# RWKV-7 and sparse-attention block on one core: half-array matmuls issued one half after the other instead of in turns

## The chip, the core and the metric

The kernel runs on one core of a Trainium2 chip. A core has a matrix engine (TensorE, PE in the profile, whose weight loads are listed apart as PEld), a vector engine (VectorE, DVE), an activation engine (ScalarE, ACT), a general engine (GpSimd, POOL) and a queue engine that issues DMAs (SyncE, SP). The metric is the device time of one launch in microseconds, the median of several runs; one execution is profiled as well.

## What is computed

One transformer block for 512 tokens of width 2048: a linear-recurrence mixer (RWKV-7, 16 heads of 64), an attention with three branches (compressed, selected, window; 16 query heads in 4 groups, head width 64), a gated mix of both, an MLP of width 8192, and RMS norms. What the change touches, cut to its core:

```
# the recurrence, per head and token; the kernel does it in chunks of 64 tokens
S = S * w_t + sa (kk_t * a_t)^T + v_t k_t^T        # sa = -S kk_t
y = S r_t

# attention, per head; q 512x64, keys and values 512x64
s = q k^T * scale - slope * dist                   # causal, masked
p = softmax(s)
o = p v                                            # gated sum of the branches
```

In chunk form the recurrence needs, for each head and chunk, the products of the scaled keys with the scaled queries (keys by queries), a triangular inverse, and two products that the text calls Z (scores times values) and W (inverse times keys).

## The kernel before

All data stands with features on the 128 partitions. Two heads of width 64 share one set of partitions: head 0 on partitions 0 to 63, head 1 on 64 to 127. Many of the products are therefore matmuls on half of the 128x128 array. There are three kinds of halves here: 64 rows of the array (a contraction over 64, written 64\*128 in the profile), 64 columns (an output of 64 partitions, 128\*64), or both (64\*64).

**Stages.** Stage 1 (`stage1`, 35 to 985 us of the span) goes over 8 pairs of heads: `gates` prepares a pair, `inner` does the work of the chunks that needs no state, `outer` runs over the 8 chunks in order. Stage 2 does the compressed keys and then `attention` (1150 to 1442 us). Stage 3 does the output projections and the MLP, 1674 us long, and the change doesn't touch it.

**Order.** PE and POOL run in the order in which the code is written. Between the pieces of `inner`, `outer` and `attention`, `pump` puts pieces of the large projections (three matmuls of 128x512 a time, L104 to L106) by a credit that the code counts, so PE has projection work to do while DVE and ACT work on the heads. DVE, ACT and SP in stage 1 and 2 are ordered by a scheduler.

**The four groups.**

- L634, in `inner_a`: keys by queries. For each half b of the 8 chunks, four chunks and two heads: the head picks the rows of the array (`hs`), and each head has an output tile of its own (`pS[h]`, named `un` in the trace). 8 pairs x 2 halves = 16 groups of 8 matmuls, 128 columns streamed each.
- L724, in `inner_b`: Z. Four pairs of chunks `cp` and the two chunks `q` of each; `q` picks rows and columns, so these are quarter arrays, 64 columns streamed. 16 groups of 8 matmuls (8 pairs, 2 heads).
- L733, in `inner_b` for the second head: W. Four `cp` and two heads; the head picks the output columns (`hs`), 128 columns streamed. 8 groups of 8 matmuls.
- L1043, in `att_c`: P V. For query tile i (0 to 3) of 128 queries, the key tiles b from 0 to i and two heads; the head picks the output columns, 128 columns streamed, and the products for all b are added up in one place. 8 pairs of heads x 2 branches x 4 tiles = 64 groups of 2(i+1) matmuls, 320 in all.

Every one of them is a matmul of f32 data, and each such matmul leaves two records in the trace (640 for the 320 of L1043), one behind the other.

Of the kernel before, what the change touches and what calls it, by code (L numbers as in the profile page):

```python
# [52 lines left out]
class Kern:  # L53
# [568 lines left out]
    def inner_a(self, cur):  # L622

        nc, p, pp = self.nc, self.p1, self.ps1
        AR, KB, S = cur["AR"], cur["KB"], cur["S"]
        sts = []
        for b in range(2):
            self.pump(PUMP["s"])
            pS = [pp.tile([128, 4, 128], F32, name="un", bufs=3) for h in range(2)]
            for i in range(4):  # L630
                c = 4 * b + i
                for h in range(2):
                    hs = slice(64 * h, 64 * h + 64)
                    nc.tensor.matmul(pS[h][:, i], KB[hs, c // 2, c % 2].rearrange("p a t -> p (a t)"),  # L634
                                     AR[hs, :, C * c:C * c + C], start=True, stop=True)
            for h in range(2):
                nc.vector.tensor_tensor(S[:, h, 4 * b:4 * b + 4].rearrange("p (a b) t -> p a b t", b=2),
                                        pS[h].rearrange("p (a b) t -> p a b t", b=2),
                                        self.mk[:, 0:2].unsqueeze(1).to_broadcast([128, 2, 2, 128]), OP.mult)
        for h in range(2):  # L640

            st = dict(h=h, NT=S[:, h, :, 0:64].rearrange("p (a b) t -> p a b t", b=2))
            X = self.masked(st, 2, F16, "X", nc.vector)
            st["DT"] = p.tile([128, 4, 128], F16, name=f"D{h}1")
            nc.vector.tensor_tensor(st["DT"], self.identb, X, OP.subtract)
            st["X"] = X
            sts.append(st)
        return sts
# [65 lines left out]
    def inner_b(self, h, cur, st):  # L714

        nc, p, pp = self.nc, self.p1, self.ps1
        S, VU, An, WT, DT = cur["S"], cur["VU"], cur["An"], cur["WT"], st["DTf"]
        hs = slice(64 * h, 64 * h + 64)
        pZ = pp.tile([128, 4, C], F32, name="un", bufs=3)
        for cp in range(4):  # L720
            for q in range(2):
                ds, ks = slice(64 * q, 64 * q + 64), slice(64 - 64 * q, 128 - 64 * q)
                c = 2 * cp + q
                nc.tensor.matmul(pZ[ds, cp], S[ks, h, c, 0:64], VU[ks, c, hs], start=True, stop=True)  # L724
        st["Z"] = p.tile([128, 4, C], F32, name="Z", bufs=1)
        nc.scalar.copy(st["Z"], pZ)
        if h == 0:
            cur["DT0"] = DT
            return
        pW = pp.tile([128, 4, 128], F32, name="un", bufs=3)  # L730
        for cp in range(4):
            for hs, dt in ((slice(0, 64), cur["DT0"]), (slice(64, 128), DT)):
                nc.tensor.matmul(pW[hs, cp], An[:, cp, hs], dt[:, cp], start=True, stop=True)  # L733
        nc.scalar.copy(WT, pW)

# [301 lines left out]
    def att_c(self, j, i, br):  # L1037
        nc = self.nc
        pT = self.pT.pop((j, i, br))
        for b in range(i + 1):  # L1040
            for h in range(2):
                v0 = 256 * br + 64 * (2 * (j // 4) + h)
                nc.tensor.matmul(self.o[j][64 * h:64 * h + 64, 128 * i:128 * i + 128], self.vn[:, b, v0:v0 + 64],  # L1043
                                 pT[h][:, b], start=False, stop=i == 3 and br == 1 and b == 3)
        if i == 3 and br == 1:
            t = self.p2.tile([128, T], F32, name="z", bufs=2)
            nc.scalar.copy(t, self.o[j])
            nc.sync.dma_start(self.yd[8 + j], t)
# [501 lines left out]
```

## Time and profile before

| | |
|---|---|
| Median of 3 runs | 3124.81 us (3119.63 to 3130.18) |
| Profiled execution, own time | 3125.73 us |
| its span, first to last instruction | 3124.0 us |
| PE busy | 3050.8 us, 98% |
| DVE, ACT, POOL busy | 1855.4, 1192.9, 588.6 us |
| DMA | 369.28 MB, mean 118 GB/s |

PE is busy nearly all the time in every one of the 40 slices. "Busy" is the union of the records of an engine: two matmul records that overlap are counted once, so a group whose mean record is long and whose busy time is short ran several at a time. "Idle before" is the time in which the engine stood still just ahead of a group, with what ended it.

### The profile page before, as it was taken

The numbers are of one execution on the slowest core, as the hardware profiler recorded it, in microseconds if no ns is written. First come the engines' busy times: TensorE is split into PE (matmuls) and PEld (weight loads), VectorE is DVE, ScalarE is ACT, GpSimd is POOL, SyncE is SP. The second block draws the span as 40 slices with busy tenths as digits, with TensorE's granted clock in tenths as the row PEclk, the third lists the DMA queues.
The fourth block names the chain that finished last, engine by engine and source line by source line (L and its number), as shares of the span: only waits on it lengthen the run. The fifth ranks groups of instructions, "written<-read, shape, count | busy, mean of one in ns | idle before, by whom it ended". The sixth has DMA issues, their size and how long they took to land.

```text
span 3124.0 us, 49657 instructions
## 1 busy us (share of the span) xinstructions
PE 3050.8 (98%) x19296; PEld 2591.8 (83%) x19296; DVE 1855.4 (59%) x3312; ACT 1192.9 (38%) x2031; POOL 588.6 (19%) x613
## 2 busy tenths in 40 slices
PE   9999999999999999999999899999999999999998
PEld 7777777777777877787888899999997888888998
DVE  7855756575563457775464877777775232344565
ACT  4322333233232335654333444444444232232454
POOL 2312222231231000001221533333330000000012
PEclk9999999999999999999999999999999999999999
DMA  4222222222224422225543344444446243253465
GB/s 163 82 85 75 82 78 74 71 82 83 77 79 142 135 95 65 65 78 189 169 144 128 133 135 128 131 135 134 128 130 204 94 139 103 94 165 118 148 193 176
DMA packets 165596, 369.28 MB, mean 118 GB/s; under 512 B 18672, under 2 KB 24304, under 8 KB 157168
## 3 DMA queue, kind: packets, MB, share of 16 engines
q1 hardware_dynamic: 154080, 339.28, 33.7%
q10 hardware_dynamic: 10640, 24.73, 2.1%
q8 instruction: 151, 2.47, 0.3%
q0 software_dynamic: 640, 2.10, 0.2%
q14 instruction: 85, 0.70, 0.1%
HBM read 322.06 MB, written 41.94 MB: 117 GB/s over the span
## 4 chain that ended last, share of the span: by engine, by line
PE 62%; DVE 2%; DMA 1%; POOL 1%; issue 0%; ACT 0%; SPq 0%; DVEq 0%; ACTq 0%; POOLq 0%
PE acc L1263 20%; PE acc L104 13%; PE acc L106 12%; PE acc L105 12%; PE po L1043 1%; PE sc L1010 1%; PE pt L1032 1%; DMA wraw<-w_down 1%; DVE wlo L68 0%; DMA u<-ud 0%; PE sc L954 0%; POOL rb L1177 0%; DMA raw<-w_up 0%; PE po L989 0%; POOL sq L1175 0%
## 5 line engine op out<-in xcount | busy, mean ns | idle before, releaser
L67 ACT CAST whi<-wraw 128x512 fp32r<-128x512 f32 x752 | 465.8, 620 | 1065.9 <-PE acc L105 989.2
L68 DVE TENSOR_TENSOR wlo<-wraw,whi 128x512 fp32r<-128x512 f32 x752 | 530.7, 707 | 567.6 <-ACT whi L67 560.0
L104 PE MATMUL acc<-xn,whi 128*128 128x512 f32 x1472 | 611.5, 415 | 1.3 <-DVE th L387 1.3
L106 PE MATMUL acc<-xn,wlo 128*128 128x512 f32 x1472 | 578.2, 393 | 0.0
L105 PE MATMUL acc<-xn,whi 128*128 128x512 f32 x1472 | 577.1, 392 | 0.0
L104 PE MATMUL acc<-xs,whi 128*128 128x512 f32 (+1 forms) x1280 | 449.5, 351 | 5.4 <-ACT xs L932 5.4
L105 PE MATMUL acc<-xs,whi 128*128 128x512 f32 (+1 forms) x1280 | 449.1, 351 | 2.0 <-DVE xs L933 2.0
L106 PE MATMUL acc<-xs,wlo 128*128 128x512 f32 (+1 forms) x1280 | 448.8, 351 | 0.1
L1263 PE MATMUL acc<-hx,hs 128*128 128x256 f32 x2048 | 369.8, 283 | 3.1 <-ACT hs L1248 3.1
L106 PEld LDWEIGHTS acc<-xn,wlo 128*128 128x128 f32 x1472 | 277.3, 188 | 61.6
L104 PEld LDWEIGHTS acc<-xn,whi 128*128 128x128 f32 x1472 | 278.1, 189 | 60.0 <-issue 6.5
L1263 PEld LDWEIGHTS acc<-hx,hs 128*128 128x128 f32 x2048 | 317.4, 190 | 3.3 <-ACT hs L1248 3.3
L105 PEld LDWEIGHTS acc<-xn,whi 128*128 128x128 f32 x1472 | 278.7, 189 | 46.0
L1263 PE MATMUL acc<-hx,ls 128*128 128x256 f32 x1024 | 289.2, 282 | 2.1 <-DVE ls L1249 2.1
L1263 PE MATMUL acc<-hx,h 128*128 128x256 f32 x1536 | 277.8, 283 | 5.0 <-ACT h L1240 5.0
L104 PEld LDWEIGHTS acc<-xs,whi 128*128 128x128 f32 x1280 | 241.4, 189 | 41.2 <-ACT xs L932 6.4
L105 PEld LDWEIGHTS acc<-xs,whi 128*128 128x128 f32 x1280 | 241.4, 189 | 38.4 <-DVE xs L933 3.5
L106 PEld LDWEIGHTS acc<-xs,wlo 128*128 128x128 f32 x1280 | 241.4, 189 | 35.5 <-DVE wlo L68 0.5
L1263 PEld LDWEIGHTS acc<-hx,h 128*128 128x128 f32 x1536 | 237.7, 190 | 5.4 <-ACT h L1240 5.4
L1249 DVE TENSOR_TENSOR ls<-s,hs 128x1024 fp32r<-128x1024 f32 x128 | 184.5, 1441 | 74.6 <-ACT hs L1248 74.5
L1263 PE MATMUL acc<-hx,l 128*128 128x256 f32 x768 | 216.5, 282 | 1.8 <-DVE l L1241 1.8
L1263 PEld LDWEIGHTS acc<-hx,ls 128*128 128x128 f32 x1024 | 195.8, 191 | 2.3 <-DVE ls L1249 2.3
(354 smaller groups left out, 4225.3 us busy)
## 6 DMA issues: line engine op xcount, KB each, us to landing
wraw<-w_down SPq DMA_DIRECT2D x320, 256.0 KB, 3.2
raw<-w_up SPq DMA_DIRECT2D x64, 1024.0 KB, 5.2
wraw<-w_gate SPq DMA_DIRECT2D x128, 256.0 KB, 3.0
wraw<-w_rkv SPq DMA_DIRECT2D x96, 256.0 KB, 3.1
wraw<-w_o SPq DMA_DIRECT2D x64, 256.0 KB, 3.1
ud<-f ACTq DMA_DIRECT2D x32, 512.0 KB, 6.2
u<-ud SPq DMA_DIRECT2D x32, 512.0 KB, 5.3
thd<-th SPq DMA_DIRECT2D x32, 256.0 KB, 3.5
```

What stands on the lines that cost most here:

```text
L67: nc.scalar.copy(hi, raw)
L68: lo_eng.tensor_tensor(lo, raw, hi.bitcast(F32), OP.subtract)
L104: nc.tensor.matmul(ps, hi[:, j], xh, start=opens and k == 0, stop=False)
L105: nc.tensor.matmul(ps, hi[:, j], xl, start=False, stop=False)
L106: nc.tensor.matmul(ps, lo[:, j], xh, start=False, stop=close and last)
L1010: nc.tensor.matmul(ps[:, 0:n], q, self.kst[h][:, x, br, 0:n], start=x == 0, stop=x == 1)
L1032: nc.tensor.transpose(pt[:, b], s[:, 128 * b:128 * b + 128], self.ident)
L1043: nc.tensor.matmul(self.o[j][64 * h:64 * h + 64, 128 * i:128 * i + 128], self.vn[:, b, v0:v0 + 64], pT[h][:, b], start=False, stop=i == 3 ...
L1249: nc.vector.tensor_tensor(l, s, h.bitcast(F32), OP.subtract)
L1263: nc.tensor.matmul(o, w[wi][part][:, 128 * i:128 * i + 128], x[:, xi, xp], start=kh == 0 and i == 0 and m == 0 and slot in opens, stop=kh ...
```

## The change

In all four groups the two loops are exchanged: the loop that picks the half of the array is now the outer one. The same matmuls run on the same data into the same places; no instruction is added or taken away.

```diff
         for b in range(2):                                  # inner_a
             pS = [pp.tile([128, 4, 128], F32, name="un", bufs=3) for h in range(2)]
-            for i in range(4):
-                c = 4 * b + i
-                for h in range(2):
+            for h in range(2):
+                for i in range(4):
+                    c = 4 * b + i
                     hs = slice(64 * h, 64 * h + 64)
                     nc.tensor.matmul(pS[h][:, i], KB[hs, c // 2, c % 2].rearrange("p a t -> p (a t)"),
                                      AR[hs, :, C * c:C * c + C], start=True, stop=True)
...
-        for cp in range(4):                                 # inner_b
-            for q in range(2):
+        for q in range(2):
+            for cp in range(4):
                 ds, ks = slice(64 * q, 64 * q + 64), slice(64 - 64 * q, 128 - 64 * q)
                 c = 2 * cp + q
                 nc.tensor.matmul(pZ[ds, cp], S[ks, h, c, 0:64], VU[ks, c, hs], start=True, stop=True)
...
-        for cp in range(4):
-            for hs, dt in ((slice(0, 64), cur["DT0"]), (slice(64, 128), DT)):
+        for hs, dt in ((slice(0, 64), cur["DT0"]), (slice(64, 128), DT)):
+            for cp in range(4):
                 nc.tensor.matmul(pW[hs, cp], An[:, cp, hs], dt[:, cp], start=True, stop=True)
...
-        for b in range(i + 1):                              # att_c
-            for h in range(2):
+        for h in range(2):
+            for b in range(i + 1):
                 v0 = 256 * br + 64 * (2 * (j // 4) + h)
                 nc.tensor.matmul(self.o[j][64 * h:64 * h + 64, 128 * i:128 * i + 128], self.vn[:, b, v0:v0 + 64],
                                  pT[h][:, b], start=False, stop=i == 3 and br == 1 and b == 3)
```

On PE, P V of query tile 3 (i = 3) of the first pair of heads, before. `po` is the output, `pT_11725` and `pT_11732` the softmax probabilities of head 0 and head 1, `vn` the values:

```order
L1032 MATMUL pt_11787<-ident_58,s_11600 128x128 x4
L1032 MATMUL pt_11794<-ident_58,s_11606 128x128 x4
L1043 MATMUL po_11243<-pT_11725,vn_9871 64x128
L1043 MATMUL po_11243<-pT_11732,vn_9871 64x128
L1043 MATMUL po_11243<-pT_11725,vn_9871 64x128
L1043 MATMUL po_11243<-pT_11732,vn_9871 64x128
L1043 MATMUL po_11243<-pT_11725,vn_9871 64x128
L1043 MATMUL po_11243<-pT_11732,vn_9871 64x128
L1043 MATMUL po_11243<-pT_11725,vn_9871 64x128
L1043 MATMUL po_11243<-pT_11732,vn_9871 64x128
L104 MATMUL acc_11740<-hn3_9861,whi_11588 128x512
```

The same place after:

```order
L1032 MATMUL pt_11787<-ident_58,s_11600 128x128 x4
L1032 MATMUL pt_11794<-ident_58,s_11606 128x128 x4
L1043 MATMUL po_11243<-pT_11725,vn_9871 64x128 x4
L1043 MATMUL po_11243<-pT_11732,vn_9871 64x128 x4
L104 MATMUL acc_11740<-hn3_9861,whi_11588 128x512
```

The four matmuls of head 0 now stand in a row, then the four of head 1; what is ahead and behind is unchanged. L634 and L733 move in the same way (`un_1272` and `un_1273` there are the outputs of the two heads), and L724 too, whose rows read alike for both halves. On DVE the scheduler answers with a small move in `inner_a` of each pair: the evacuations of keys by queries (L637, `S`), and what is made of them for the inverse (L652 `X`, L645 `D`; 0 and 1 are the heads), beside a piece of the projections' weights (L68):

```order
 L637 TENSOR_TENSOR S_1263<-un_1296,masks_753 128x512
+L652 TENSOR_TENSOR X0_1308<-S_1263,masks_753 128x512
 L637 TENSOR_TENSOR S_1263<-un_1297,masks_753 128x512
-L652 TENSOR_TENSOR X0_1308<-S_1263,masks_753 128x512
+L645 TENSOR_TENSOR D01_1310<-ident_58,X0_1308 128x512
 L652 TENSOR_TENSOR X1_1312<-S_1263,masks_753 128x512
-L645 TENSOR_TENSOR D01_1310<-ident_58,X0_1308 128x512
+L68 TENSOR_TENSOR wlo_1324<-wraw_1322,whi_1323 128x512
 L645 TENSOR_TENSOR D11_1314<-ident_58,X1_1312 128x512
-L68 TENSOR_TENSOR wlo_1324<-wraw_1322,whi_1323 128x512
```

Head 0's steps come ahead of head 1's evacuation, and one weight split moves ahead of the last step of head 1. ACT, POOL and SP keep their order.

## Rows read from the trace of the kernel before

**Rows 1.** The page: busy time by engine; granted clock over 40 slices.

```profile
PE 3050.8 (98%) x19296; PEld 2591.8 (83%) x19296; DVE 1855.4 (59%) x3312; ACT 1192.9 (38%) x2031; POOL 588.6 (19%) x613
...
PEclk9999999999999999999999999999999999999999
```

**Rows 2.** Busy time in stage 1 and in the attention; columns as named.

```profile
core 0: us, PE busy (x) PEld busy (x) DVE busy (x) ACT busy (x) POOL busy (x), PEclk, DMA share, GB/s
35.00:985.00 950.00, 926.87 (x6017) 715.99 (x6016) 586.82 (x1160) 293.78 (x548) 241.83 (x338) 1.00 0.25 82
...
1130.00:1450.00 320.00, 313.88 (x2058) 252.76 (x2058) 220.93 (x769) 175.95 (x487) 15.54 (x19) 1.00 0.26 83
```

**Rows 3.** What PE waited for: us in total, times, longest; attention, then stage 1.

```profile
PE sc L954 <- DVE sm L1012: 3.5, 7, 0.6
...
PE big L619 <- ACT sq L612: 13.8, 10, 3.9
PE un L677 <- DVE D L689: 3.3, 12, 0.3
PE un L677 <- DVE D L663: 1.3, 1, 1.3
```

**Rows 4.** Groups by line: shapes, count, busy us, mean ns, idle before.

```profile
L1043 PE MATMUL po<-pT,vn 128*64 128x128 f32 x640 | 49.1, 283 | 0.0
L1032 PE MATMUL pt<-ident,s 128*128 128x128 f32 x320 | 45.6, 273 | 0.0
```

**Rows 5.** Timeline of PE, P V: start us, us, engine, line, records; three places.

```profile
1300.09 1.09 PE L1043 MATMUL po<-pT,vn 128*64 128x128 f32 x16
1301.11 0.50 PE L104 MATMUL acc<-hn,whi 128*128 128x512 f32 x1
...
1305.90 0.44 PE L1043 MATMUL po<-pT,vn 128*64 128x128 f32 x4
1306.27 0.50 PE L104 MATMUL acc<-xn,whi 128*128 128x512 f32 x1
...
1313.01 0.66 PE L1043 MATMUL po<-pT,vn 128*64 128x128 f32 x8
1313.60 0.50 PE L104 MATMUL acc<-xn,whi 128*128 128x512 f32 x1
```

**Rows 6.** Timeline of PE in `outer`, and of the compressed keys (L888).

```profile
162.75 0.29 PE L572 MATMUL py<-S,VU 128*64 128x64 f32 x4
...
164.55 0.43 PE L550 MATMUL seq<-M,WT 128*64 128x128 f32 x2
...
1006.46 0.42 PE L888 MATMUL po<-h,cw 128*64 128x31 f32 x4 [0.34 <-ACT kbd L890]
```

**Rows 7.** Timeline of PE in `inner`: L702, then Z (L724) and W (L733).

```profile
149.33 1.11 PE L702 MATMUL un<-Df,N 128*128 128x128 f32 x8
150.19 0.48 PE L104 MATMUL acc<-xn,whi 128*128 128x512 f32 x1
...
154.99 0.68 PE L724 MATMUL un<-VU,S 64*64 64x64 f32 x16
155.60 1.09 PE L733 MATMUL un<-Q,An 128*64 128x128 f32 x16
156.63 0.51 PE L104 MATMUL acc<-xn,whi 128*128 128x512 f32 x1
```

**Rows 8.** Timeline of PE, keys by queries (L634), and of DVE there.

```profile
114.87 1.16 PE L634 MATMUL un<-AR,KB 64*128 64x128 f32 x16
115.96 0.50 PE L104 MATMUL acc<-xn,whi 128*128 128x512 f32 x1
...
121.15 1.28 DVE L645 TENSOR_TENSOR D<-ident,X 128x512 f16<-128x512 f32 x2
122.36 0.68 DVE L68 TENSOR_TENSOR wlo<-wraw,whi 128x512 fp32r<-128x512 f32 x1
```

**Rows 9.** What ended DVE's waits at L637, whole span: us, times, longest.

```profile
DVE S L637 <- PE un L634: 11.5, 10, 1.4
```

**Rows 10.** Stretches around a drop of the granted clock; columns as in rows 2.

```profile
437.60:439.40 1.80, 0.57 (x5) 0.57 (x6) 0.07 (x1) 1.24 (x3) 0.40 (x2) 0.97 0.37 133
439.40:443.00 3.60, 3.60 (x11) 2.81 (x11) 3.60 (x7) 0.42 (x1) 0.00 (x0) 0.54 0.26 84
```

## Prediction

> **What bounds the kernel now.** I read the busy times first. PE is busy 3050.8 of 3124.0 us, the next engine 59% [rows 1], and the two stages that the change touches look the same: PE 926.87 of 950 us in stage 1, 313.88 of 320 us in the attention [rows 2]. Then PE's waits: in the attention the largest is 3.5 us in all, in stage 1 it is 13.8 us at L619, behind a chain of small operations at the end of each pair of heads, and a few us at L677 [rows 3]. So PE's own time sets the end here, its order is written by hand, and a microsecond that a group on PE takes longer is a microsecond of the end, unless it stands in a place where PE would have waited anyway.
>
> **How fast the groups run now.** Line sums show something odd: P V (L1043) has 640 records of mean 283 ns in only 49.1 us, the transposes (L1032), with as many columns streamed, have 320 records of mean 273 ns in 45.6 us [rows 4]. Twice the records in about the same time: two halves of the array work at once. The timeline gives the price. A group of 16 records starts at 1300.09 and the next matmul at 1301.11, 1.02 us; a group of 4 takes 1305.90 to 1306.27, 0.37 us [rows 5]. Twelve records more cost 0.65 us. I call one turn, in which each half takes one record, a step: six more steps, 0.108 us each, and 0.37 - 2 x 0.108 = 0.15 us that a group pays once. A whole-array f32 matmul with the same columns, L702, takes 149.33 to 150.19 for 8 records, 0.1075 us each [rows 7]. So a step of two halves costs what one record costs on the whole array; the second half rides for free.
>
> The other groups read likewise. W (L733): 155.60 to 156.63, 1.03 us for 16 records, the same 0.108 a step. Z (L724): 154.99 to 155.60, 0.61 us; less 0.15, by 8 steps, 0.058 us (at most 0.61/8 = 0.076) [rows 7]. Keys by queries (L634): 114.87 to 115.96, 1.09 us [rows 8]; less 0.15 that is 0.1175 a step, and L702's 0.1075 is the floor; I take 0.112.
>
> **What the change does to that.** It removes and adds nothing. Within a half the records were one behind the other before, too, so the price of a step for one half is known from the same rows. What changes is who stands next to whom. With n matmuls per half, before there were 2n steps (two records each, both halves together). After, half A's 2n records stand ahead of half B's. If nothing of them overlaps, there are 4n steps; if all of it does, still 2n. The question is how far PE lets a matmul of the other half pass matmuls that wait for their own half.
>
> Three rows bear on it. Two records of one half alone, L550, take 0.43 us from first start to last end, and four records of two halves, the 4-record group of L1043, take 0.44 us [rows 5, 6]. In the second case the program's order is A, B, and each is two records. Were B's first record held until A's second had begun, the group would have three steps, 0.108 us more. It has two: B passes at least one waiting record of A, so two neighbouring matmuls of different halves overlap whole. And four records of one half, L888, take 0.42 us with 31 columns, where four records of two halves, L572, take 0.29 us with 64 columns [rows 6]: within one half nothing overlaps.
>
> In the new order A and B are neighbours once in each group: A's last matmul and B's first. By what the rows show, those two overlap, and the other n - 1 of each half run alone. A group then has 2n + 2(n - 1) steps, 2(n - 1) more than before. That is my forecast:
>
> - L634, n = 4: 16 groups x 6 steps x 0.112 = 10.8 us.
> - L724, n = 4: 16 x 6 x 0.058 = 5.6 us (7.3 at 0.076).
> - L733, n = 4: 8 x 6 x 0.108 = 5.2 us.
> - L1043, n = i + 1: for each of 16 (pair, branch) 0 + 2 + 4 + 6 = 12 steps, 16 x 12 x 0.108 = 20.7 us. At i = 0 the order doesn't change.
>
> Sum 42.3 us, half in stage 1 and half in the attention.
>
> What could take some of it back: PE's waits in these stages. L619 comes after a chain that begins behind `inner`, so its 13.8 us stay. The 3.5 us at L954, where PE waits for DVE to empty a score tile, can shrink, since DVE gains slack; L677 with 4.6 us likewise [rows 3]. At most 8 us, likeliest near nothing, since the extra work stands behind these waits' causes and not between cause and wait. DVE gets head 0's scores earlier than head 1's and its waits at L637 (11.5 us in 10 times [rows 9]) move, but it is busy only 586.82 of the 950 us of stage 1 [rows 2]. In DVE's new order a weight split, 0.68 us, stands ahead of the last `D` of head 1 [rows 8]; that `D` is first used behind `pump` with some five pieces of projection of 0.7 us, which hide it. Without that cover it would be 8 x 0.68 = 5.4 us. I take zero for each, and -8 to +5 us into the range.
>
> The profiled execution took 3125.73 us, 0.9 us over the median; 3125.7 + 42.3 - 0.9 = 3167 us.
>
> **Rivals.**
>
> *Hardly any overlap at the border.* A's last records may be under way before B's first is looked at. Then L634 pays 8 steps a group (14.3 us), L724 7.4, L733 6.9, and L1043 4 + 6 + 8 = 18 steps for i = 1 to 3, 31.1 us: 60 us, 3185. With one record overlapping, about 51 us. For it: nothing in the trace shows the border itself. Against it: the 4-record group. The Trainium skill, "TensorE: Matmul & The Clock Gate", Part 3 (The mechanism), states that matmuls start and end strictly in program order and only weight loads are pulled ahead; by that rule this rival would hold, but the 4-record group, 0.44 us against 0.43 us of two records, disagrees with it.
>
> *The two halves still run together; not slower.* If PE looks far ahead, B's first record starts beside A's first, although seven records of A (n = 4) stand between them. Every group keeps its 2n steps and the change does nothing: 0 us, 3125, with -4 for DVE's earlier start. It decides at the depth of that look: with 7 waiting records passed all groups are whole, with 3 passed the groups of n = 2 are whole, and n = 4 pays 4 steps instead of 6, n = 3 two: 7.2 + 3.7 + 3.5 + 16 x 6 x 0.108 = 24.8 us, 3150. For it: B demonstrably passes one record. Against it: no row shows more than one, because before A and B never stand further apart. The same page's table of TensorE's queue gives it a depth of 64 and a partial reorder window; taken at its word for matmuls, it would give this rival's 3125, and no run here shows it.
>
> *The clock falls.* In 439.40 to 443.00 the granted clock was 0.54, the lower of the two levels (1.2 instead of 2.4 GHz), behind a stretch in which PE was busy 0.57 of 1.80 us [rows 10]; that cost about 3.6 x 0.46 = 1.7 us. If PE at work with half of its array let the clock fall too, each of the 32 long groups of the attention could bring it, 54 us beside the 42: 3221. Against it: PE stays busy in all of them, L1043 runs beside whole-array work, and the page's clock is near full everywhere [rows 1].
>
> *Faster by more than the noise.* Head 0's scores are done half a group earlier. The gain is bounded by PE's waits at L677, 4.6 us, so it can't be seen.
>
> **How the numbers follow.** Forecast (border of one matmul, 3159 to 3174): 0.42. Hardly any overlap (3175 to 3188): 0.20. Deeper look, part of the cost (3138 to 3158): 0.12. Full overlap (3121 to 3130): 0.21. Clock: 0.03. Anything faster by over 0.3%: 0.02. About 0.3%, 9.4 us, is what a measurement of this kernel can tell from no change. So slower 0.42 + 0.20 + 0.12 + 0.03 = 0.77, same 0.21, faster 0.02. Without the full overlap the range would leave out 0.26, so it reaches there: 3121 to 3188; given that the kernel gets slower at all, I expect 3148 to 3188.
>
> **What would show it.** The mean record of the four lines stays (283 ns for P V); the busy time of L1043 goes from 49.1 to about 70 us (49 by the full overlap, 80 without any). A 16-record group of L1043 goes from 1.02 to 1.67 us (1.02 by full overlap, 1.88 with none at the border), L634 from 1.09 to 1.76, L733 from 1.03 to 1.68, L724 from 0.61 to 0.96, and the 4-record group stays at 0.37. The 8-record group (n = 2, 0.59 us from 1313.01 to 1313.60 [rows 5]) decides the depth: 0.81 us by the forecast, unchanged if B passes three records. Stage 3 and the waits of PE stay within a few us. I am wrong if the groups lengthen and the end doesn't move as much, for then PE's time was not the bound, or if a wait of another engine on these groups grows beside them.

## The result: 0.93% slower, seven tenths of the forecast

The changed kernel takes 3153.65 us in the median of 4 runs (3151.15 to 3157.55), against 3123.82 us of the kernel before (3119.63 to 3130.18): 1.0093 times as long, 95% interval 1.008 to 1.0106, or 29.8 us more. The forecast was 3167 us with a range of 3121 to 3188. The direction was right, and so was what bounds the kernel, PE's own time; the size was 13 us too large, because PE overlaps the two halves further than the forecast had it.

The page of the changed kernel, its busy times and the granted clock, beside [rows 1]:

```profile
span 3149.4 us, 49651 instructions
...
PE 3078.2 (98%) x19296; PEld 2619.6 (83%) x19296; DVE 1856.8 (59%) x3312; ACT 1193.5 (38%) x2031; POOL 589.1 (19%) x613
...
PEclk9999999999999999999999999999999999999999
```

The same number of matmul records keeps PE busy 27.4 us longer, and the span is 25.4 us longer. The other engines do what they did. The four groups, first as they were before (shapes, count, busy us, mean ns of one, idle before; L1043 stands in [rows 4]):

```profile
L634 PE MATMUL un<-AR,KB 64*128 64x128 f32 x256 | 18.7, 285 | 0.0
L724 PE MATMUL un<-VU,S 64*64 64x64 f32 x256 | 10.9, 224 | 0.0
L733 PE MATMUL un<-Q,An 128*64 128x128 f32 x128 | 8.8, 279 | 0.0
```

and in the changed kernel:

```profile
L1043 PE MATMUL po<-pT,vn 128*64 128x128 f32 x640 | 61.3, 283 | 0.0
...
L634 PE MATMUL un<-AR,KB 64*128 64x128 f32 x256 | 27.4, 285 | 0.0
L724 PE MATMUL un<-VU,S 64*64 64x64 f32 x256 | 15.4, 224 | 0.0
L733 PE MATMUL un<-Q,An 128*64 128x128 f32 x128 | 12.6, 279 | 0.0
```

Read the two numbers behind the bar together. No matmul takes longer (283, 285, 224 and 279 ns as before), but the time in which at least one is at work grows by 12.2, 8.7, 4.5 and 3.8 us, 29.2 us in all: fewer of them run side by side. The waits of PE are nearly as in [rows 3]; here those of the attention (us in total, times, longest) and, below, of stage 1:

```profile
PE sc L954 <- DVE sm L1012: 3.5, 7, 0.6
...
PE big L619 <- ACT sq L612: 14.0, 10, 3.9
PE un L677 <- DVE D L689: 3.3, 12, 0.3
PE un L677 <- POOL X L652: 0.3, 1, 0.3
```

So next to nothing was taken back by waits: of [rows 3] only the single wait of 1.3 us at L677, for DVE's `D` of L663, is gone, and 0.3 us for POOL stands in its place. Up to the last matmul of the recurrence (L572) PE stood still for 27.1 us, 28.2 before. By stage it adds up as well: that matmul starts at 965.1 instead of 948.8 us, 16.3 later, where the three groups ahead of it are 17.0 longer, and P V takes from 1174.9 to 1465.6 instead of 1160.1 to 1438.9, 11.9 more, where its groups are 12.2 longer. The stretches between and behind these two, which the edit doesn't touch, are 1.5 and 1.3 us shorter in this execution; that is why the two spans differ by 25.4 us and not by the 28.2 of these two stages.

How long one group now takes, from the timeline of PE (start us, us, engine, line, records), to be held against [rows 5], [rows 7] and [rows 8]:

```profile
113.90 1.71 PE L634 MATMUL un<-AR,KB 64*128 64x128 f32 x16
115.54 0.50 PE L104 MATMUL acc<-xn,whi 128*128 128x512 f32 x1
...
155.34 0.96 PE L724 MATMUL un<-VU,S 64*64 64x64 f32 x16
156.24 1.58 PE L733 MATMUL un<-Q,An 128*64 128x128 f32 x16
157.75 0.50 PE L104 MATMUL acc<-xn,whi 128*128 128x512 f32 x1
...
1315.70 1.58 PE L1043 MATMUL po<-pT,vn 128*64 128x128 f32 x16
1317.21 0.50 PE L104 MATMUL acc<-hn,whi 128*128 128x512 f32 x1
...
1333.60 0.66 PE L1043 MATMUL po<-pT,vn 128*64 128x128 f32 x8
1334.20 0.50 PE L104 MATMUL acc<-xn,whi 128*128 128x512 f32 x1
...
1342.00 1.14 PE L1043 MATMUL po<-pT,vn 128*64 128x128 f32 x12
1343.07 0.50 PE L104 MATMUL acc<-xn,whi 128*128 128x512 f32 x1
```

From each start to the start of the next matmul: L634 1.64 us (1.09 before), L724 0.90 (0.61), L733 1.51 (1.03), P V with 16 records 1.51 (1.02), with 12 records 1.07 (0.81; from here on a figure without a fence is read from the timeline in the same way), with 8 records 0.60 (0.59). The 8-record group is the same to within 0.01 us, and the 16-record group lost 4.5 steps of 0.109 us, not six.

### The profile page after: what moved, and what is told of

It reads as the page before. It is cut to its first block, busy times and chain, and to the rows that moved or that the text cites. A ratio compares the mean times of both kernels' runs of the same rounds, so it can differ in the third digit from the quotient of the medians.

```text
span 3149.4 us, 49651 instructions
## 1 busy us (share of the span) xinstructions
PE 3078.2 (98%) x19296; PEld 2619.6 (83%) x19296; DVE 1856.8 (59%) x3312; ACT 1193.5 (38%) x2031; POOL 589.1 (19%) x613
## 4 chain that ended last, share of the span: by engine, by line
PE 61%; DVE 2%; DMA 1%; POOL 1%; ACT 0%; issue 0%; SPq 0%; DVEq 0%; ACTq 0%; POOLq 0%
PE acc L1263 20%; PE acc L104 12%; PE acc L106 12%; PE acc L105 12%; PE po L1043 2%; PE sc L1010 1%; PE pt L1032 1%; DMA wraw<-w_down 1%; DVE wlo L68 0%; DMA u<-ud 0%; PE sc L954 0%; POOL rb L1177 0%; PE po L989 0%; ACT whi L67 0%; DMA raw<-w_up 0%
## 5 line engine op out<-in xcount | busy, mean ns | idle before, releaser
L68 DVE TENSOR_TENSOR wlo<-wraw,whi 128x512 fp32r<-128x512 f32 x752 | 529.5, 705 | 575.0 <-ACT whi L67 567.2
```

Source lines behind the costliest of these rows:

```text
L68: lo_eng.tensor_tensor(lo, raw, hi.bitcast(F32), OP.subtract)
```

## Where the second half starts

The records of one 16-record group of P V, counted in stretches that begin at its start (columns: the stretch, its length, PE busy and the records in it, clock, DMA):

```profile
1315.69:1316.17 0.48, 0.47 (x4) 1.00 0.00 0
1315.69:1316.21 0.52, 0.51 (x6) 1.00 0.00 0
```

Up to 1316.17 four records have begun, in the trace 0, 0.16, 0.27 and 0.38 us after the first: head 0 alone. Within the next 0.04 us two more begin, one of which is the fifth of head 0, since its four so far came one at a time; the other is the first of head 1 (it takes 323 ns, as the first record of the group does, all others 272 or 273). At that moment the sixth, seventh and eighth record of head 0 have not begun, and head 1 has passed them. In the 8-record group (four records a half) head 1 begins with head 0:

```profile
1333.59:1333.70 0.11, 0.10 (x2) 1.00 0.00 0
```

In both a matmul of the other half passes three records that wait; in the long group, where seven stand between it and head 0's first, it passes no more than three. I call this the depth theory. It makes a price for every order: with r records in a row for each half, the first r - 4 of the first half run alone, and so do the last r - 4 of the second; and since the second half's first load could not be hidden beside the first half's, half a step more in L1043 and L733, nearly a whole one in L634 and L724. That fits the three group sizes of P V (0, 2 and 4 steps, and 0.5 with the last two). Its rivals in the runs that follow: the forecast's, that two neighbouring matmuls of different halves overlap (border); that the second half starts a fixed time behind the first (time); and that a fixed share of the overlap is lost (share).

## Experiments

**The halves in blocks of two.** In all four groups two matmuls of one half are followed by two of the other; for P V:

```diff
-        for b in range(i + 1):
-            for h in range(2):
+        for b0 in range(0, i + 1, 2):
+            for h, b in ((h, b) for h in range(2) for b in range(b0, min(b0 + 2, i + 1))):
```

> All four groups in blocks of two matmuls: two of one half, two of the other, and so on (for P V of three key tiles: two, two, one, one). Theory depth: a matmul of the other half may pass up to three waiting records, which is what stands between the first records of two neighbouring blocks here. Then every group keeps its steps as in the kernel before: 1.09 us for L634, 0.61 for L724, 1.02 for L733 and for the 16-record group of L1043, and the time is that of before within 3 us. Theory border (the forecast's: only two neighbouring matmuls of different halves overlap): groups of four per half pay two steps more, those of three and two per half in L1043 two as well; together 17.6 us more than before, about 3141 us. Theory time (the other half starts a fixed time of about half a microsecond behind the first): L634 at about 1.6 us, the whole at about 3150 us.

Measured: 3128.63 against 3124.22 us, ratio 1.0012 (1.0003 to 1.0021), so 4 us more, where the border theory wanted 17.6 and the time theory some 25. The line groups:

```profile
L1043 PE MATMUL po<-pT,vn 128*64 128x128 f32 x640 | 50.1, 284 | 0.0
L634 PE MATMUL un<-AR,KB 64*128 64x128 f32 x256 | 20.2, 290 | 0.0
L724 PE MATMUL un<-VU,S 64*64 64x64 f32 x256 | 11.7, 227 | 0.0
L733 PE MATMUL un<-Q,An 128*64 128x128 f32 x128 | 9.2, 282 | 0.0
```

The groups together are 3.7 us longer than before, 1.0, 1.5, 0.8 and 0.4. That is a miss of the depth theory as I wrote it, which said none, by a small term: where a second block of two follows, half a step, or nearly a whole one in L634 and L724, is lost in the middle of the group (a 16-record group of P V takes 1.07 us instead of 1.02, L634 1.19 instead of 1.09). The depth decides almost all; the two halves need not be issued strictly in turns.

**P V alone, and the three groups of stage 1 alone.** Each is the corresponding part of the change's diff.

> Only P V (L1043) head by head, the three groups of stage 1 as before. Theory (PE's own time is the end, and each group's own loss adds up): the 16-record group of L1043 at 1.51 us, the 12-record one at 1.07, those of 8 and 4 as before, 12.2 us more in all, and the end later by that much, about 3136 us; stage 1 ends where it ended before. Rival (some of it is taken back by PE's waits in the attention): the groups as long, the end later by less than 9 us.

> Only the three groups of stage 1 (L634, L724, L733) half by half, P V as before. Theory (own time, adding up): L634 at 1.64 us, L724 at 0.90, L733 at 1.51; 8.6 + 4.5 + 3.9 = 17.0 us more, about 3141 us, and with the run of P V alone the two make up the whole change. Rival (part of it goes into waits): less than 13 us at the end.

Measured, P V alone: 3133.68 us, ratio 1.0036 (1.0022 to 1.005), 9.5 us more, with an interval of some 7 to 16. The other three: 3138.52 us, ratio 1.0047 (1.0032 to 1.0062), 14.3 us more, interval 10 to 19. The groups themselves came out exactly; P V alone, then the three alone:

```profile
L1043 PE MATMUL po<-pT,vn 128*64 128x128 f32 x640 | 61.3, 283 | 0.0
L634 PE MATMUL un<-AR,KB 64*128 64x128 f32 x256 | 18.7, 285 | 0.0
```

```profile
L1043 PE MATMUL po<-pT,vn 128*64 128x128 f32 x640 | 49.1, 283 | 0.0
L634 PE MATMUL un<-AR,KB 64*128 64x128 f32 x256 | 27.4, 285 | 0.0
```

Both medians lie a little under the sum of their groups; P V alone is clear of the rival's 9 us by half a microsecond only, the other three of their rival's 13 us by 1.3, and the intervals exclude neither. The profiles do. With the three groups alone the last matmul of the recurrence starts at 965.0 us, 16.2 later than before, and the wait of 1.3 us at L677 is gone here too: a microsecond of 17.0 is all that waits gave back. In the profile of P V alone, P V took from 1156.9 to 1447.7 us, 12.0 longer than before: the attention gave nothing back. But it began 3.2 us earlier than before, at a place that the edit doesn't touch. The trace shows why (the stretch, its length, PE busy and records, granted clock; before, then P V alone):

```profile
985.00:1075.00 90.00, 87.77 (x451) 0.96 0.45 142
```

```profile
985.00:1075.00 90.00, 87.75 (x466) 1.00 0.46 147
```

In the compressed keys the clock fell to its lower level (1.2 instead of 2.4 GHz) twice in one execution and not in the other, and PE did 15 records fewer in the 90 us. These drops come and go between executions and are worth a few microseconds at the end; a difference of 3 us of two profiled executions means nothing here, and the busy time of the groups is the better measure. By it the two halves of the change make 12.2 + 17.0 us, the whole 29.2.

**Keys by queries twice over, in turns and head by head.** The first decides the price of a step, the second what happens with 16 records in a row.

```diff
-            for i in range(4):
+            for i in list(range(4)) * 2:      # in turns; head by head: this loop inside that over h
```

> Keys by queries (L634) issued twice over, the two heads in turns: 16 matmuls a group instead of 8, the second eight overwrite the same values. Both theories: eight steps more a group, 1.09 + 8 x 0.1115 = 1.98 us, 16 x 0.89 = 14.3 us over the kernel before.

> Keys by queries (L634) issued twice over, head 0's eight matmuls and then head 1's eight. Theory depth (at the border the second half passes three waiting records, however many stand ahead): 16 steps of head 0 less 4 shared, plus 16, and nearly one more for the first load of head 1: 1.98 + 12.9 x 0.1115 = 3.42 us a group, 23 us over the run in turns. Theory time (head 1 starts a fixed 0.55 us behind head 0): 1.98 + 0.55 = 2.53 us a group, 9 us over. Theory share (a constant part, 0.6, of the shared steps is lost): 1.98 + 9.8 x 0.1115 = 3.07 us, 17 us over.

Measured: 3134.83 and 3164.17 us, one run each, beside 3123.66 us of the kernel before. A group of each in the timeline:

```profile
117.68 2.06 PE L634 MATMUL un<-AR,KB 64*128 64x128 f32 x32
119.67 0.50 PE L104 MATMUL acc<-xn,whi 128*128 128x512 f32 x1
```

```profile
119.17 3.50 PE L634 MATMUL un<-AR,KB 64*128 64x128 f32 x32
122.59 0.50 PE L104 MATMUL acc<-xn,whi 128*128 128x512 f32 x1
```

1.99 us in turns (1.98 expected) and 3.42 us head by head (3.42 by depth, 2.53 by time, 3.07 by share). What is lost grows with the length of the run, by one step for each record beyond four that a half has. Time and share are out. (The run in turns was 11 us over the kernel before, where its groups say 14, and head by head 29 us over the run in turns, where 23 were expected. Up to the last matmul of the recurrence the traces have 13.6 and 23.5 us; the rest arises behind it, in stages that the edit doesn't touch.)

**One record for each matmul.** P V on 16-bit floats, in turns and head by head; each matmul then leaves one record, and a step is half as long, 0.056 us.

```diff
-            self.vn = p.tile([128, 4, 512], F32, name="vn")
+            self.vn = p.tile([128, 4, 512], F16, name="vn")
...
-            pT = p.tile([128, 4, 128], F32, name="pT", bufs=4)
+            pT = p.tile([128, 4, 128], F16, name="pT", bufs=4)
```

> P V (L1043) on 16-bit floats (values and probabilities are rounded to 16 bits, so this part is less exact), the heads in turns: one record for each matmul instead of two. Theory depth and theory border alike: 320 records; a group of i = 3 has 4 steps of about 0.055 us and 0.15 once, 0.37 us. About 26 us less than before.

> The same with P V head by head. Between the first records of the two heads there now stand at most three records (i = 3). Theory depth, counted in records: the second head passes all of them, no group gets longer and the time is that of the run in turns within 3 us. If the depth were counted in matmuls of the program (two f32 matmuls are what the second half passed at most): i = 3 pays two steps and i = 2 one, about 0.11 and 0.055 us a group, 2.6 us in all, and the 8-record group takes 0.48 instead of 0.37 us. Theory border: i = 3 pays three steps, 0.54 us a group.

Measured: 3098.94 and 3102.57 us, one run each. The 3.6 us between them are 0.6 more than I allowed, and not in P V, whose busy time is 21.2 and 21.7 us; head by head the granted clock was 0.50 from 1274.0 to 1280.8 us, 1.00 in turns, and PE began 24 records there instead of 47: half of 6.8 us is 3.4, by estimate nearly all of it. What brought that drop isn't shown. The lines of P V, in turns and then head by head:

```profile
L1043 PE MATMUL po<-pT,vn 128*64 128x128 f16 x320 | 21.2, 229 | 0.0
```

```profile
L1043 PE MATMUL po<-pT,vn 128*64 128x128 f16 x320 | 21.7, 231 | 0.0
...
1185.35 0.42 PE L1043 MATMUL po<-pT,vn 128*64 128x128 f16 x8
1185.71 0.50 PE L104 MATMUL acc<-hn,whi 128*128 128x512 f32 x1
```

The group of i = 3 takes 0.36 us here, 0.34 in turns (0.37 expected). Four matmuls of f32 data in a row cost 0.49 us, four of 16-bit data 0.01: it is records that count, not matmuls of the program. The border theory, which wanted 0.54 us, is out.

**Is it three records, or the time of three?** In 16 bits a record is half as long, so a limit in time would let six pass. The first key tile is issued again at the head of each group, once or as often as there are tiles. The edit below has the inner loop of both runs head by head, one line for each; the run in turns has the first of the two as its outer loop and the heads inside.

```diff
-        for b in range(i + 1):
-            for h in range(2):
+        for h in range(2):
+            for b in [0, *range(i + 1)]:                       # one more
+            for b in [0] * (i + 1) + [*range(i + 1)]:          # or as many more
```

> P V on 16-bit floats, heads in turns, with the product of the first key tile issued once more at the head of each group (so that tile counts twice in the output): 2 to 5 records for each head. All theories: one step more than the 16-bit run in turns in each of the 64 groups, the group of i = 3 takes 0.344 + 0.056 = 0.40 us.

> The same (first key tile counted twice) head by head: at i = 3 five records of head 0 stand ahead of head 1's first, at i = 2 four, of which three wait while the first runs. Theory depth, three waiting records whatever the type: i = 0 to 2 as in turns (0.23, 0.29, 0.35 us), i = 3 pays one step and the first load again, 0.48 us instead of 0.40. If three was not the limit for 16-bit records (a depth in time or in columns: three f32 records are 0.33 us, six 16-bit ones): i = 3 at 0.41 too. If it is two matmuls of the program: i = 2 at 0.46.

> P V on 16-bit floats head by head with as many repeats of the first key tile as there are tiles (it counts i + 2 times in the output): 2, 4, 6, 8 records for each head. Theory depth: i = 0 and 1 as in turns (0.23, 0.35 us), i = 2 pays two steps and the load, 0.46 + 0.11 + 0.03 = 0.60 us, i = 3 four, 0.57 + 0.22 + 0.03 = 0.82 us. Depth in time (0.33 us): i = 2 as in turns, 0.46, i = 3 two steps, 0.70.

The timeline of the run in turns (five records for each head), of the second run (four and five) and of the third (six and eight):

```profile
1186.12 0.47 PE L1043 MATMUL po<-pT,vn 128*64 128x128 f16 x10
1186.52 0.50 PE L104 MATMUL acc<-hn,whi 128*128 128x512 f32 x1
```

```profile
1179.48 0.42 PE L1043 MATMUL po<-pT,vn 128*64 128x128 f16 x8
1179.83 0.50 PE L104 MATMUL acc<-hn,whi 128*128 128x512 f32 x1
...
1187.84 0.55 PE L1043 MATMUL po<-pT,vn 128*64 128x128 f16 x10
1188.32 0.50 PE L104 MATMUL acc<-hn,whi 128*128 128x512 f32 x1
```

```profile
1180.07 0.66 PE L1043 MATMUL po<-pT,vn 128*64 128x128 f16 x12
1180.66 0.50 PE L104 MATMUL acc<-hn,whi 128*128 128x512 f32 x1
...
1189.01 0.89 PE L1043 MATMUL po<-pT,vn 128*64 128x128 f16 x16
1189.83 0.50 PE L104 MATMUL acc<-hn,whi 128*128 128x512 f32 x1
```

With four records the group takes 0.35 us (0.34 in turns); with five 0.48, where in turns it takes 0.40; with six 0.59 and with eight 0.82 us. All four were expected to within 0.01 us by three waiting records, and a limit in time wanted 0.41, 0.46 and 0.70 for the last three. Whether PE counts matmuls or pairs of a weight load and a matmul can't be told apart: each of the 19296 matmul records has one load. The times at the end were 3100.55 (in turns), 3101.92 and 3113.56 us, one run each.

**A version faster than both.** The run on 16-bit floats in turns was timed again.

> P V on 16-bit floats in turns again (values and probabilities rounded to 16 bits), timed against the kernel before: the groups of P V are 27.9 us shorter in the profile (44.6 to 16.7 us), so about 3096 to 3100 us. Theory own time: the ratio is 0.991 to 0.993. Rival (the attention would wait for DVE or ACT instead): above 0.996.

3100.87 against 3125.65 us, ratio 0.992 (0.9903 to 0.9936). It gives up some exactness of one product, so it is not the same bargain; but as an experiment it shows the other sign of the same thing. P V's groups got shorter by 27.9 us and the end came 24.8 us earlier (20 to 30 by the interval). The rival was wrong as to the size, but it was there: the stretch of P V, before and in this run (its length, PE busy and records, clock), and what PE waited for in this run, to be held against [rows 3]:

```profile
1160.10:1438.90 278.80, 274.95 (x1872) 1.00 0.23 73
...
1160.80:1417.00 256.20, 248.41 (x1552) 0.99 0.25 83
...
PE sc L954 <- DVE sm L1012: 6.2, 7, 1.2
```

The stretch is 22.6 us shorter, not 27.9: PE stood still for 7.8 us of it instead of 3.9, since it now waits longer for DVE, and the clock fell once. So PE's own time sets the end wholly when P V gets longer, and most of it when P V gets shorter.

## Why the prediction was right, and its size not

The measured 3154 us lies outside the band of the forecast itself (3159 to 3174) and in the one to which the prediction gave a chance of 0.12 (3138 to 3158, the deeper look). It is inside the stated range because that range was drawn to cover the rivals as well.

- *PE is the bound, and its microseconds add up.* Right: 29.2 us more in the groups, 29.8 us in the medians (25 to 33 by the interval), 1 us less in PE's waits.
- *The price of a step.* Right: 0.109 us for P V and W, 0.058 for Z, 0.1115 for keys by queries (I had 0.108, 0.058 and 0.112).
- *Within one half nothing overlaps.* Right: one record each 0.109 us in the first 0.48 us of the group above.
- *At the border the last matmul of A overlaps the first of B, and no more.* This is the step that failed. I took what the rows of before showed as the most that PE does, though they could only show the least: with the halves in turns, a matmul never had to pass more than one waiting record. It passes three. So a group of four matmuls for each half pays 4 steps and not 6, of three 2 and not 4, of two none and not 2. The 8-record group, which the prediction had named as the sign, decided it: 0.60 us, where the forecast wanted 0.81. The rival that I called the deeper look had exactly these steps, 24.8 us for the sum.
- *What no rival had:* the second half's first load. Each half begins with a gap wider than a step (0.16 instead of 0.109 us in L1043 and L733, 0.11 instead of 0.058 in L724, 0.21 instead of 0.1115 in L634). In turns both halves pay it at once; in a row the second pays it where the first is already running, half a step for L1043 and L733, nearly one for L634 and L724. That makes 24.8 into 29.2 us. That the gap is the load's is argued, not shown: it exceeds a step by 0.05 us where a half loads 64 columns of weights and by 0.10 us in L634, where it loads 128, but no run varies the load alone.
- *The rival "hardly any overlap", with the strict order of matmuls that the Trainium skill states* ("TensorE: Matmul & The Clock Gate", Part 3, The mechanism): the trace disagrees. In the changed kernel all eight records of head 0 stand ahead of head 1's first in the program, and head 1's first begins when five of them have. Across halves of the array a later matmul does start ahead of an earlier one; so PE doesn't start its matmuls strictly in the order in which the code is written either.
- *The rival "full overlap":* the groups with two matmuls for each half did just that, to within 0.01 us, and the 16-bit ones with four. The same page of the Trainium skill gives, in its table at the top, a queue 64 deep with a partial reorder window for weight loads; the prediction took it for matmuls. It is no help further out: in these runs three waiting pairs of load and matmul were the limit.
- *The clock.* It didn't fall in the half-array groups: 1.00 from 1170 to 1470 us, all of P V. In stage 1 of the changed kernel it was at its lower level from 443.9 and from 884.3 us, for some 3.4 us each (0.51 and 0.50), each time behind a wait of PE at L619 (3.9 and 2.5 us) and over whole-array matmuls. [rows 10] has the first of these drops; the second also stands in the run on 16-bit floats in turns (0.50 from 870.6 us), where stage 1 is unchanged.
- *DVE's changed order and its waits:* hardly any effect. PE waits 3.6 us at L677 instead of 4.6; the difference, the 1.3 us for L663, is gone in both runs with the new order in stage 1; with blocks of two it is there (1.2 us).

## What to carry to other kernels

If matmuls on different parts of the array are independent, issue them near each other: by these runs, with not more than three waiting records between the first of one part and the first of the other; and remember that an f32 matmul is two records. Strict turns are not needed (blocks of two f32 matmuls for each half cost 0.1%), but whole loops over one half, then the other, cost one step for every record beyond the fourth. Count times mean duration over busy time is how a profile shows such overlap, and how it shows that it's gone; but hold it against a whole-array group, whose records overlap a little too: 1.9 for the transposes [rows 4], 3.7 for P V before and 3.0 after.

## What the runs showed of the hardware that I had not expected

- Matmuls of a part of the array that is free start ahead of matmuls that stand earlier in the program and wait for their own part, but past three of them only, whether a record streams 128 columns in 0.109 us (f32), 64 in 0.058 us, or 128 in 0.056 us (16 bits), and whether the parts differ in rows (L634), in columns (L733, L1043) or in both (L724).
- The drops of the granted clock in the compressed keys (0.96 in one execution and 1.00 in another, over 90 us) differ between executions of code that is the same there; there they put off the attention by about 3 us.
